# S5 generator: additions moved between VectorE, GpSimd and accumulating DMAs

## The chip, the core and the metric

The kernel runs on one NeuronCore of a Trainium2 chip. The metric is the device time of one launch in microseconds (us). Three runs of the kernel before gave 1716.67, 1719.01 and 1724.01 us, with a median of 1719.01 us. The profiled execution took 1714.45 us. Engines are named as in the profile: PE is TensorE (PEld its weight load), DVE is VectorE, ACT is ScalarE, POOL is GpSimd and SP is SyncE, which issues most of the DMAs.

## The reference, cut to what matters

The reference is one step of a four-layer trunk over 384 tokens (128 of a context, 256 of a sample): an S5 layer, a retention layer, a Hyena layer and a second S5 layer. The change lies in the S5 layers, nearly all of it in the first.

```python
# s5_branch: per layer j; 64 groups of 16 channels, state of 64 complex lanes, two directions
proj = h @ w_in
u, gate = proj[..., :1024], proj[..., 1024:]
bb = f * b                       # complex; f from lam and the step
bu = einsum('blgh,gph->blgp', u, bb)
h[t] = a * h[t-1] + bu[t]        # scan over time, forwards and backwards
y = Re(einsum('blgp,ghp->blgh', h, c)) + d_skip * u
g = gelu(y)
y = g * sigmoid(g @ w_glu + b_glu)
out = (y * silu(gate)) @ w_out
```

## The kernel before, in words

Time is cut into 48 chunks of 8 steps, for each group of channels. Inside a chunk the layer is a small Toeplitz matrix (`Tm`, read back from the scratch array `kd`). Between chunks the state is carried by a recurrence. So for each of 16 "half blocks" (`hb`, four groups each) a generator makes three things out of tables of powers (`B1`, `BI`, `F1`, `FI`): the state input matrices `BP`, which PE transposes into `PB`, the rows of the Toeplitz matrix `Kc`, and the state output matrices `CP`. Each of these is a complex product that `expand` (L625) makes for one direction as two multiplications and one addition over a 128x512 tile: `out = c1*x0` (L629), `t = c2*x1` (L630), `out = out + t` (L631). The second product goes to the ring `xt`. The addition goes through the helper `gstt` to POOL, and so shows in the profile under the helper's line, L134.

The first S5 layer (`j == 0`) runs in these stretches, in this order:

1. **Generator and input projection** (L807 to L822, after the string `PLAN0`). `get_p` calls `gen_b1` (L637) and `gen_b2` (L654) for each half block. DVE multiplies, POOL adds, PE makes the Toeplitz rows (L663) and the transposes (L669), ACT copies out, DVE adds the skip term to `Kc` (L674, L675). Between them the four U weights (1 MB each) are split into a high and a low part (`unit`, L156: ACT casts `wh`, DVE or POOL subtracts to get `wl`, as `sub_any` shares it out) and multiplied with the normalised input `h`. `h` itself is split by `put` (L174), whose subtraction `hl` runs on POOL here (`adanorm(i, hpool, G)`). Six of the 16 `CP` (`SPL`) are made here as well, in a single buffer, and spilled to the scratch array `cpd` by a DMA that POOL issues (L645).
2. **Recurrences** (`recur`, L768). Two halves of the state (`Xs`, q = 0 and 1), for each of 47 dependent steps of five DVE instructions over 128x64 (L790 to L794). Meanwhile PE works through the gate projection (`dense`, L834), whose low parts are all made by POOL (`pool_share[0] = PSG`, which is 3).
3. **Read-out** (L858 to L904). For eight channel blocks m, PE adds three products, one with `Tm` (L878) and two with `CP` (L879, L880), then ACT and DVE apply GELU. The ten `CP` that were not spilled are generated here by `gen_c` (L682): those of m = 0 and 1 (`CPG` is 2) wholly on POOL, the others with DVE multiplications and POOL additions. The other six are loaded back. `xt` has two buffers here and three in the first stretch, and `CP` has six.
4. **GLU and output projection** (L924 to L927), then the retention layer, in which the matrices of the second S5 layer are generated bit by bit, with additions on POOL.

The order of instructions on each engine is fixed when the program is built, by a scheduler that works from its own timeline of the program. Each engine takes its instructions strictly in that order, so an instruction that waits holds back all that stand behind it.

Of the kernel before, what the change touches and what calls it, by code (L numbers as in the profile page):

```python
# [14 lines left out]
OP = mybir.AluOpType  # L15
# [19 lines left out]
RB = 7  # L35
NBC = 2
NH = 2
CPG = 2
RB1 = 10
CP1 = 6  # L40
QS = ("gpsimd", "gpsimd")
# [22 lines left out]
PS0 = 1  # L64
# [41 lines left out]
def hybrid_trunk(ctx: ExitStack, tc: tile.TileContext, I, O, dbg=None, layers=(0, 1, 2, 3)):  # L106
    nc = tc.nc
    V, S, G, TE = nc.vector, nc.scalar, nc.gpsimd, nc.tensor
# [13 lines left out]
    def psm():  # L122
        return pm.tile([128, 512], F32, tag="m", name="psm")
# [9 lines left out]
    def gstt(out, a, b, op):  # L133
        G.tensor_tensor(out, a, b, op=op)  # L134
# [7 lines left out]
    pool_share = [1]  # L142
# [275 lines left out]
    def first_ssq():  # L418
        pss = ssq["first"] = [psm() for _ in range(3)]
        for fb in range(NB):  # L420
            sq = t384("sq")
            S.activation(sq, xT[:, fb, :], AF.Square)
            for t in range(3):
                TE.matmul(pss[t][:, :2], sq[:, t * 128:(t + 1) * 128], ones[:, 0:2], start=fb == 0, stop=fb == NB - 1)
# [197 lines left out]
            defer.extend(steps)  # L622
        return dict(B1=B1, BI=BI, F1=F1, FI=FI, sgn=sgn, dsk=dsk, dmask=dmask)

    def expand(out, rot, T1, T2, x, sl, l0, bufs, eng):  # L625
        c1 = T1[:, sl, l0:l0 + 4].rearrange("p e l -> p l e").unsqueeze(3).to_broadcast([128, 4, 8, 16])
        c2 = T2[:, sl, l0:l0 + 4].rearrange("p e l -> p l e").unsqueeze(3).to_broadcast([128, 4, 8, 16])
        t = rot.tile([128, 4, 8, 16], F32, tag="xt", name="xt", bufs=bufs)
        eng.tensor_tensor(out, c1, x[:, 0].unsqueeze(2).to_broadcast([128, 4, 8, 16]), op=OP.mult)  # L629
        eng.tensor_tensor(t, c2, x[:, 1].unsqueeze(2).to_broadcast([128, 4, 8, 16]), op=OP.mult)  # L630
        gstt(out, out, t, OP.add)  # L631

    def expand_c(CP, rot, tb, xc, hb, xb, eng):
        for d in range(2):
            expand(CP[:, d], rot, tb["B1"], tb["BI"], xc[:, d], slice(1, 9) if d == 0 else slice(8, 0, -1), d * 64 + hb * 4, xb, eng)

    def gen_b1(j, hb, tb, rot, xb=3, nb=1, spill=False):  # L637
        if hb % nb == 0:
            tb["bc"] = rot.tile([128, nb, 2, 2, 2, 4, 16], F32, tag="bc", name="bc", bufs=2)
            (nc.gpsimd if hb > 2 else nc.sync).dma_start(tb["bc"], I["s5bc"][j, hb // 4, :, hb % 4:hb % 4 + nb])  # L640
        rb, xc = tb["bc"][:, hb % nb, 0], tb["bc"][:, hb % nb, 1]
        if spill:
            CP = rot.tile([128, 2, 4, 8, 16], F32, tag="CP", name="CP", bufs=1)
            expand_c(CP, rot, tb, xc, hb, xb, V)
            getattr(nc, SPQ).dma_start(I["cpd"][hb], CP.rearrange("p d g e c -> p (d g e c)"))  # L645
        S.activation(xc, xc, AF.Copy, scale=tb["sgn"][:, 1:2])
        BPs = []
        for d in range(2):
            BP = rot.tile([128, 4, 8, 16], F32, tag="BP", name="BP", bufs=max(xb, 2))
            expand(BP, rot, tb["F1"], tb["FI"], rb[:, d], slice(7, None, -1) if d == 0 else slice(0, 8), d * 64 + hb * 4, xb, V)  # L650
            BPs.append(BP)
        return BPs, xc

    def gen_b2(j, hb, tb, rot, ops, ring=None):  # L654
        BPs, xc = ops
        PB = (ring or rot).tile([128, 4, 2, 128], F32, tag="PB", name="PB")
        psk = psm()
        bps = [[BP[:, g].rearrange("p a b -> p (a b)") for g in range(4)] for BP in BPs]
        last = None
        for d in range(2):  # L660
            xcf = xc[:, d].rearrange("p a b c -> p (a b c)")
            for g in range(4):
                last = TE.matmul(psk[32 * g:32 * g + 32, d * 128:(d + 1) * 128], xcf[:, g * 16:g * 16 + 32], bps[d][g],  # L663
                                 start=True, stop=True)
        with tc.issue_after(last.ins):
            for d in range(2):
                ps = psm()
                for g in range(4):
                    TE.transpose(ps[:, g * 128:(g + 1) * 128], bps[d][g], ident)  # L669
                S.copy(PB[:, :, d, :], ps.rearrange("p (g c) -> p g c", c=128))  # L670
        Kc = rot.tile([128, 240], F32, tag="Kc", name="Kc")
        S.copy(Kc[:, 0:128], psk[:, 0:128])
        S.copy(Kc[:, 128:240], psk[:, 144:256])
        V.tensor_add(Kc[:, 112:128], Kc[:, 112:128], psk[:, 128:144])  # L674
        V.scalar_tensor_tensor(Kc[:, 112:128], tb["dmask"], tb["dsk"][:, hb:hb + 1], Kc[:, 112:128], op0=OP.mult, op1=OP.add)  # L675
        kdm = I["kd"][j * 8 + hb // 2]
        nc.scalar.dma_start(bass.AP(tensor=kdm.tensor, offset=kdm.offset + (hb % 2) * 960, ap=[[240, 4], [1920, 32], [1, 240]]), Kc)
        if ring is None:
            nc.scalar.dma_start(I["pbd"][hb], PB.rearrange("p g d c -> p (g d c)"))
        return PB  # L680

    def gen_c(j, hb, tb, rot, CP, xb, eng=V):  # L682
        xc = rot.tile([128, 2, 2, 4, 16], F32, tag="xc", name="xc")
        nc.sync.dma_start(xc, I["s5bc"][j, hb // 4, :, hb % 4, 1])
        expand_c(CP, rot, tb, xc, hb, xb, eng)

    def gen_cs(j, hb, tb, rot):
        CP = rot.tile([128, 2, 4, 8, 16], F32, tag="CP", name="CP")
# [7 lines left out]
    def s5(i, j, nxt, begun=lambda: None):  # L696
        def mk(st, name, bufs=1, **kw):
            return st.enter_context(tc.tile_pool(name=f"{name}_{i}", bufs=bufs, reuse_waits="tile", **kw))
# [7 lines left out]
        hpool = mk(ep, "s5h")  # L706
        h0 = load(pool, "h0", I["s5h0"][j], eng=nc.scalar)
        if j == 0:
# [3 lines left out]
            with ExitStack() as e2:  # L712
                tb = gen_setup(j, tpool, fpool, mk(e2, "s5p"))
        if i == 0:
            first_ssq()
        h = adanorm(i, hpool, G)
        if j == 1:
            gates = deque(mods(i, 8, 12))
            for _ in range(KN3):
# [87 lines left out]
        for op in (PLAN0, PLAN1)[j].split():  # L807
            n = int(op[1:])
            if op[0] == "A":
                ahead(n)  # L810
            elif op[0] == "U":
                if j == 0:
                    pool_share[0] = PS0 if n == 0 else 1
                firstmajor(i, weight(I["s5_w_in"][j, n]), h, u_epi, 2 * n)
                if n == 0:
                    begun()
            elif op[0] == "P":
                use_p(n)
            elif op[0] == "R":
                recur(n)  # L820
            else:
                tick(n)  # L822
# [17 lines left out]
        rot = mk(e2, "s5c", 2)  # L840
# [17 lines left out]
        for m in range(8):  # L858
            CP = []
            for r in range(2):  # L860
                c = rot.tile([128, 2, 4, 8, 16], F32, tag="CP", name="CP", bufs=CPB if j == 0 else CP1)
                if j == 0 and 2 * m + r not in SPL:
                    gen_c(j, 2 * m + r, tb, rot, c, 2, G if m < CPG else V)
                else:
                    (CQ if j else nc.sync).dma_start(c.rearrange("p d g e c -> p (d g e c)"), I["cpd"][2 * m + r])
                CP.append(c)
# [539 lines left out]
    rb, _ = rstd_bcast()  # L1406
    rs = t384("rs")
    S.copy(rs, rb[:, :T])
    for fb in range(NB):
        t = xT[:, fb, :]  # L1410
# [164 lines left out]
```

## Time and profile before

| | |
|---|---|
| median of three runs | 1719.01 us |
| profiled execution, its own time | 1714.45 us |
| its span on the core | 1712.6 us |
| PE busy | 1500.0 us (88%), 10370 matmuls |
| DVE busy | 1323.1 us (77%), 3065 instructions |
| ACT busy | 686.5 us (40%) |
| POOL busy | 760.9 us (44%), 542 instructions |
| DMA | 253.02 MB, mean 148 GB/s |

The span is the time from the first to the last instruction of the program. The profiled execution's own time is 1.85 us longer than its span. Busy times are shares of that span. They are averages over stretches with different limits: the first S5 layer lies between about 28 and 475 us, the retention layer up to about 760 us, the Hyena layer up to about 1350 us, and the second S5 layer fills the rest.

### The profile page before, as it was taken

How to read it: one execution, taken by the hardware profiler on the slowest of the kernel's cores; microseconds unless marked ns; L12 is line 12 of the kernel's file. 1: busy time of each engine (PE TensorE's matmuls, PEld its weight loads, DVE VectorE, ACT ScalarE, POOL GpSimd, SP SyncE). 2: the span in 40 equal slices, each digit the busy share in tenths (PEclk: the TensorE clock that was granted, in tenths of full speed). 3: DMA queues.
4: the chain of work that ended last, by engine and by line, in shares of the span. 5: the costliest groups of instructions: out<-in, count | busy, mean ns of one | idle time of the engine just before them, and what ended most of it. 6: DMA issues, size and time to landing. Idle time of an engine off the chain costs nothing. (4 is left out here: it accounts for less than half of the span.)

```text
span 1712.6 us, 27808 instructions
## 1 busy us (share of the span) xinstructions
PE 1500.0 (88%) x10370; PEld 1330.8 (78%) x10370; DVE 1323.1 (77%) x3065; ACT 686.5 (40%) x1275; POOL 760.9 (44%) x542
## 2 busy tenths in 40 slices
PE   5788664998779999999979999999999998976996
PEld 3466454877679888889969988989999797775996
DVE  8986999889596776765867888888798764399355
ACT  2434320333324343334445545455454444521343
POOL 2866262424165657461225566556666131230221
PEclk9888796998889999999989999999999999987998
DMA  8476273554545555542432222222222463755431
GB/s 343 134 239 218 64 180 115 191 173 168 194 165 177 172 206 177 191 177 88 163 126 96 96 74 96 96 90 81 96 90 76 147 234 109 230 151 177 125 123 62
DMA packets 103199, 253.02 MB, mean 148 GB/s; under 512 B 28023, under 2 KB 68056, under 8 KB 83480
## 3 DMA queue, kind: packets, MB, share of 16 engines
q1 hardware_dynamic: 80768, 200.12, 35.8%
q0 software_dynamic: 7376, 26.48, 4.7%
q10 hardware_dynamic: 14920, 24.65, 4.0%
q8 instruction: 82, 1.34, 0.3%
q14 instruction: 53, 0.43, 0.1%
HBM read 220.37 MB, written 30.83 MB: 147 GB/s over the span
## 5 line engine op out<-in xcount | busy, mean ns | idle before, releaser
L134 POOL TENSOR_TENSOR wl<-wr,wh 128x1024 fp32r<-128x1024 f32 (+2 forms) x101 | 253.2, 2507 | 361.6 <-ACT wh L162 309.5
L162 ACT CAST wh<-wr 128x1024 fp32r<-128x1024 f32 (+4 forms) x211 | 215.5, 1029 | 339.4 <-PE psd L139 222.2
L139 PE MATMUL psd<-hh,wh 128*128 128x384 f32 x880 | 309.2, 353 | 47.8 <-DVE sgate L532 23.1
L139 PE MATMUL psd<-hh,wl 128*128 128x384 f32 x880 | 307.0, 350 | 15.9 <-DVE wl L149 8.2
L139 PE MATMUL psd<-hl,wh 128*128 128x384 f32 x880 | 307.1, 349 | 5.8 <-DVE hl L470 4.8
L139 PEld LDWEIGHTS psd<-hh,wh 128*128 128x128 f32 x880 | 171.4, 195 | 60.8 <-issue 44.2
L149 DVE TENSOR_TENSOR wl<-wr,wh 128x1024 fp32r<-128x1024 f32 (+3 forms) x110 | 144.6, 1316 | 71.6 <-ACT wh L162 71.2
L139 PEld LDWEIGHTS psd<-hh,wl 128*128 128x128 f32 x880 | 170.5, 194 | 25.5 <-DVE wl L149 10.1
L139 PEld LDWEIGHTS psd<-hl,wh 128*128 128x128 f32 x880 | 171.2, 195 | 16.4 <-DVE hl L470 7.5
L134 POOL TENSOR_TENSOR CP<-CP,xt 128x512 f32<-128x512 f32 x64 | 95.6, 1499 | 90.6 <-DVE xt L630 72.2
L134 POOL TENSOR_TENSOR BP<-BP,xt 128x512 f32<-128x512 f32 x64 | 96.6, 1514 | 80.0 <-DVE xt L630 30.6
L139 PE MATMUL psd<-wh,hh 128*128 128x256 f32 x384 | 111.7, 295 | 4.7 <-ACT k L1074 4.1
L139 PE MATMUL psd<-wl,hh 128*128 128x256 f32 x384 | 111.5, 292 | 4.1 <-POOL wl L134 2.2
L139 PE MATMUL psd<-wh,hl 128*128 128x256 f32 x384 | 110.5, 289 | 0.0
L139 PE MATMUL psd<-zb,wh 128*128 128x384 f32 x240 | 81.1, 339 | 0.0
L139 PEld LDWEIGHTS psd<-wl,hh 128*128 128x128 f32 x384 | 75.7, 197 | 5.9 <-DVE wl L149 3.0
L139 PEld LDWEIGHTS psd<-wh,hh 128*128 128x128 f32 x384 | 74.7, 196 | 6.6 <-ACT k L1074 4.9
L630 DVE TENSOR_TENSOR xt<-FI,bc 128x512 f32<-128x512 f32 x64 | 64.4, 1018 | 16.8 <-POOL CP L134 9.1
L139 PEld LDWEIGHTS psd<-wh,hl 128*128 128x128 f32 x384 | 75.5, 197 | 0.3 <-issue 0.2
L791 DVE TENSOR_TENSOR m<-X,A 128x64 f32<-128x64 f32 x188 | 69.4, 369 | 0.0
L630 DVE TENSOR_TENSOR xt<-BI,xc 128x512 f32<-128x512 f32 x44 | 47.4, 1077 | 26.6 <-POOL CP L134 18.4
L379 PE MATMUL psn<-wr,sgc 128*32 128x256 f32 x640 | 52.5, 404 | 16.3 <-DMA wr<-in_mod_w_dram 9.9
(388 smaller groups left out, 4020.9 us busy)
## 6 DMA issues: line engine op xcount, KB each, us to landing
wr<-in_mod_w_dram SPq DMA_DIRECT2D x40, 1024.0 KB
wr<-in_hy_w_in_dram SPq DMA_DIRECT2D x32, 1024.0 KB
wr<-in_ret_w_in_dram SPq DMA_DIRECT2D x24, 1024.0 KB
wr<-in_s_w_in_dram SPq DMA_DIRECT2D x16, 1024.0 KB
wm<-in_mod_w_dram SPq DMA_DIRECT2D x8, 1024.0 KB
Tt<-scratch_kd_dram SPq DMA_DIRECT2D x128, 64.0 KB
wr<-in_s_w_glu_dram SPq DMA_DIRECT2D x8, 1024.0 KB
wr<-in_s_w_out_dram SPq DMA_DIRECT2D x8, 1024.0 KB
```

The lines of the kernel that those rows point to most:

```text
L134: G.tensor_tensor(out, a, b, op=op)
L139: TE.matmul(out, lhs[a], rhs[b], start=start and i == 0, stop=stop and i == len(combos) - 1)
L149: V.tensor_sub(out, a, b)
L162: S.copy(hi, ap)
L379: TE.matmul(ps[q * 32:(q + 1) * 32, :256], sg[:, kb, 6 - 2 * u:38 - 2 * u], raw[:, kb, :], start=u == 0 and k2 == 0, stop=u == 3 and k2 == 1)
L630: eng.tensor_tensor(t, c2, x[:, 1].unsqueeze(2).to_broadcast([128, 4, 8, 16]), op=OP.mult)
L791: V.tensor_mul(m1, cur, A1)
```

## The change

There are five edits.

- `expand` is told where its addition runs: on an engine that is named, or, with `None`, in an accumulating DMA that POOL issues (`dma_start(out, t, accum_op=add)`, SBUF to SBUF, 128x512 float32, 256 KB).
- The `BP` additions of the first S5 layer run on DVE; those made in the retention layer for the second S5 layer stay on POOL (`G if j else V`).
- The `CP` additions of the first S5 layer, spilled or not, become accumulating DMAs. The multiplications that POOL made for m = 0 and 1 go to DVE, and `CPG` is gone. `gen_cs`, which makes the `CP` of the second layer, keeps its additions on POOL.
- The first layer's `hl` subtractions run on DVE, and so do all eight U splits (`pool_share[0] = 0`).
- `Kc`: ACT copies 112 columns rather than 128, and DVE makes the diagonal block from PSUM directly (first the skip term, then the second direction's block).

```diff
-    def expand(out, rot, T1, T2, x, sl, l0, bufs, eng):
+    def expand(out, rot, T1, T2, x, sl, l0, bufs, eng, add):
...
         eng.tensor_tensor(out, c1, x[:, 0].unsqueeze(2).to_broadcast([128, 4, 8, 16]), op=OP.mult)
         eng.tensor_tensor(t, c2, x[:, 1].unsqueeze(2).to_broadcast([128, 4, 8, 16]), op=OP.mult)
-        gstt(out, out, t, OP.add)
+        if add is None:
+            nc.gpsimd.dma_start(out, t, accum_op=OP.add)
+        else:
+            add.tensor_tensor(out, out, t, op=OP.add)
...
-            expand_c(CP, rot, tb, xc, hb, xb, V)
+            expand_c(CP, rot, tb, xc, hb, xb, V, None)
...
-            expand(BP, rot, tb["F1"], tb["FI"], rb[:, d], slice(7, None, -1) if d == 0 else slice(0, 8), d * 64 + hb * 4, xb, V)
+            expand(BP, rot, tb["F1"], tb["FI"], rb[:, d], slice(7, None, -1) if d == 0 else slice(0, 8), d * 64 + hb * 4, xb, V, G if j else V)
...
-        S.copy(Kc[:, 0:128], psk[:, 0:128])
+        S.copy(Kc[:, 0:112], psk[:, 0:112])
         S.copy(Kc[:, 128:240], psk[:, 144:256])
+        V.scalar_tensor_tensor(Kc[:, 112:128], tb["dmask"], tb["dsk"][:, hb:hb + 1], psk[:, 112:128], op0=OP.mult, op1=OP.add)
         V.tensor_add(Kc[:, 112:128], Kc[:, 112:128], psk[:, 128:144])
-        V.scalar_tensor_tensor(Kc[:, 112:128], tb["dmask"], tb["dsk"][:, hb:hb + 1], Kc[:, 112:128], op0=OP.mult, op1=OP.add)
...
-    def gen_c(j, hb, tb, rot, CP, xb, eng=V):
+    def gen_c(j, hb, tb, rot, CP, xb, eng=V, add=G):
...
-        h = adanorm(i, hpool, G)
+        h = adanorm(i, hpool, V if j == 0 else G)
...
-                    pool_share[0] = PS0 if n == 0 else 1
+                    pool_share[0] = 0
...
-                    gen_c(j, 2 * m + r, tb, rot, c, 2, G if m < CPG else V)
+                    gen_c(j, 2 * m + r, tb, rot, c, 2, V, None)
```

On POOL, at the start of the generator (right behind the last product of the power tables, `pb`), the row before is full of additions (`BP`, `CP`), `h` splits (`hl`) and weight splits (`wl`):

```order
L134 TENSOR_TENSOR BP<-BP,xt 128x512 x3
L176 TENSOR_TENSOR hl<-hf,hh 128x384 x3
L134 TENSOR_TENSOR BP<-BP,xt 128x512 x2
L176 TENSOR_TENSOR hl<-hf,hh 128x384 x3
L640 DMA bc<-in_s5bc_dram 128x1024
L134 TENSOR_TENSOR BP<-BP,xt 128x512 x2
L176 TENSOR_TENSOR hl<-hf,hh 128x384 x2
L134 TENSOR_TENSOR CP<-CP,xt 128x512 x2
```

With the change POOL at the same place only issues DMAs: loads of `bc` (the generator's input), accumulations into `CP`, and the spill behind each pair of them:

```order
L642 DMA bc<-in_s5bc_dram 128x1024
L631 DMA CP<-xt 128x512 x2
L642 DMA bc<-in_s5bc_dram 128x1024
L647 DMA scratch_cpd_dram<-CP 128x1024
L631 DMA CP<-xt 128x512 x2
L647 DMA scratch_cpd_dram<-CP 128x1024
```

All POOL arithmetic of that stretch has moved to DVE, but for the additions into `CP`, which have become DMAs in POOL's row.

On DVE, in the first stretch of the generator, the row before has only products (`xt`), the normalisation (`ht`) and the skip term (`Kc`):

```order
L395 SCALAR_TENSOR_TENSOR sc_145<-mod_144,vec 128x16
L630 TENSOR_TENSOR xt<-FI,bc 128x512
L460 TENSOR_TENSOR ht<-xT,psm 128x384
L630 TENSOR_TENSOR xt<-FI,bc 128x512
L460 TENSOR_TENSOR ht<-xT,psm 128x384
```

With the change the additions into `BP` and the `hl` subtractions stand between them:

```order
L394 SCALAR_TENSOR_TENSOR sc_145<-mod_144,vec 128x16
L629 TENSOR_TENSOR xt<-FI,bc 128x512
L633 TENSOR_TENSOR BP<-BP,xt 128x512 x2
L459 TENSOR_TENSOR ht<-xT,psm 128x384
L633 TENSOR_TENSOR BP<-BP,xt 128x512
L629 TENSOR_TENSOR xt<-FI,bc 128x512
L175 TENSOR_TENSOR hl<-hf,hh 128x384
```

Between the start of this stretch and the first instruction of the first recurrence the row of DVE grows by 28 additions, 8 subtractions and 2 weight splits.

On DVE, in the recurrences (`X_200` and `X_201` are the two halves of the state, `sw` and `m` their products), the row before reaches the first products of `CP` only near the end of the second recurrence, behind the last gate block:

```order
L532 SCALAR_TENSOR_TENSOR sgate<-silu,psd 128x384
L790 STREAM_SHUFFLE sw<-X_201 128x64
L791 TENSOR_TENSOR m_2510<-X_201,A_399 128x64
L793 TENSOR_TENSOR sw<-sw,A_399 128x64
L792 TENSOR_TENSOR X_201<-X_201,m_2510 128x2x32
L794 TENSOR_TENSOR X_201<-X_201,sw 128x2x32
L790 STREAM_SHUFFLE sw<-X_201 128x64
L791 TENSOR_TENSOR m_2517<-X_201,A_399 128x64
L793 TENSOR_TENSOR sw<-sw,A_399 128x64
L792 TENSOR_TENSOR X_201<-X_201,m_2517 128x2x32
L794 TENSOR_TENSOR X_201<-X_201,sw 128x2x32
L629 TENSOR_TENSOR CP<-B_224,xc 128x512 x2
```

With the change they begin while both recurrences are still running, before the fourth gate block:

```order
L792 STREAM_SHUFFLE sw<-X_200 128x64
L793 TENSOR_TENSOR m_1874<-X_200,A_399 128x64
L628 TENSOR_TENSOR CP<-B_224,xc 128x512
L629 TENSOR_TENSOR xt<-BI,xc 128x512
L796 TENSOR_TENSOR X_201<-X_201,sw 128x2x32
L628 TENSOR_TENSOR CP<-B_224,xc 128x512
L629 TENSOR_TENSOR xt<-BI,xc 128x512
L796 TENSOR_TENSOR X_201<-X_201,sw 128x2x32
L795 TENSOR_TENSOR sw<-sw,A_399 128x64
L794 TENSOR_TENSOR X_200<-X_200,m_1874 128x2x32
L531 SCALAR_TENSOR_TENSOR sgate<-silu,psd 128x384
```

Up to the last instruction of the second recurrence the row before has 8 products of this kind; with the change it has 39, four additions into `BP` and four GELU blocks in place of two.

## Rows read from the trace of the kernel before

**Rows 1.** Windows: stretch; length, busy PE, PEld, DVE, ACT, POOL; clock, DMA share, GB/s.

```profile
47.00:178.00 131.00, 99.70 (x844) 70.72 (x844) 108.33 (x132) 55.22 (x126) 90.52 (x64) 0.85 0.62 202
178.00:231.00 53.00, 41.70 (x322) 31.45 (x323) 53.00 (x301) 16.68 (x33) 11.11 (x8) 0.83 0.31 88
231.00:267.00 36.00, 12.99 (x83) 10.62 (x81) 36.00 (x45) 6.16 (x11) 35.81 (x28) 0.78 0.55 127
267.00:318.00 51.00, 37.28 (x302) 32.03 (x303) 50.09 (x268) 8.59 (x17) 7.71 (x6) 0.82 0.54 163
318.00:355.00 37.00, 36.47 (x351) 30.81 (x348) 25.68 (x52) 11.77 (x23) 16.48 (x12) 1.00 0.59 201
```

**Rows 2.** Timeline, DVE: start and length; the recurrences' first and last instruction.

```profile
178.29 1.24 DVE L773 COPY XF<-X 128x32 f32<-128x32 f32 x1
...
317.82 0.26 DVE L794 TENSOR_TENSOR X<-X,sw 128x64 f32<-128x64 f32 x1
```

**Rows 3.** Groups, DVE, 47 to 178 us: busy, mean ns | idle before.

```profile
L630 DVE TENSOR_TENSOR xt<-FI,bc 128x512 f32<-128x512 f32 x29 | 35.1, 1239 | 0.7 <-POOL BP L134 0.7
L629 DVE TENSOR_TENSOR BP<-F,bc 128x512 f32<-128x512 f32 x30 | 26.8, 914 | 7.3 <-PE psm L669 7.3
L630 DVE TENSOR_TENSOR xt<-BI,bc 128x512 f32<-128x512 f32 x12 | 14.2, 1197 | 1.3 <-DMA bc<-in_s5bc_dram 1.3
L675 DVE SCALAR_TENSOR_TENSOR Kc<-dmask,dsk,Kc 128x16 f32<-128x16 f32 x13 | 13.9, 1071 | 0.1
L629 DVE TENSOR_TENSOR CP<-B,bc 128x512 f32<-128x512 f32 x12 | 8.0, 682 | 9.0 <-DMA bc<-in_s5bc_dram 9.0
L149 DVE TENSOR_TENSOR wl<-wr,wh 128x1024 fp32r<-128x1024 f32 x4 | 6.1, 1519 | 0.0
```

**Rows 4.** One line's instructions, whole span: ns min/median/max, first and last start.

```profile
L630 DVE TENSOR_TENSOR xt<-FI,bc x64: 675/693/3122, 51.4 to 747.3; 128x512 f32<-128x512 f32 x64
...
L629 DVE TENSOR_TENSOR BP<-F,bc x64: 644/684/1780, 47.3 to 741.3; 128x512 f32<-128x512 f32 x64
...
L675 DVE SCALAR_TENSOR_TENSOR Kc<-dmask,dsk,Kc x32: 214/366/3540, 60.6 to 755.9; 128x16 f32<-128x16 f32 x32
...
L176 DVE TENSOR_TENSOR zl<-zz,zh x16: 546/554/1026, 374.1 to 1666.4; 128x384 fp32r<-128x384 f32 x16
```

**Rows 5.** Groups, POOL, 47 to 178 us.

```profile
L134 POOL TENSOR_TENSOR BP<-BP,xt 128x512 f32<-128x512 f32 x29 | 45.7, 1585 | 25.7 <-DVE BP L629 14.6 <-DVE xt L630 6.0 <-DVE Kc L674 2.8
```

**Rows 6.** Groups, DVE, 231 to 266 us, while POOL is busy throughout.

```profile
L794 DVE TENSOR_TENSOR X<-X,sw 128x64 f32<-128x64 f32 x8 | 12.1, 1559 | 0.0
L793 DVE TENSOR_TENSOR sw<-sw,A 128x64 f32<-128x64 f32 x7 | 9.7, 1387 | 0.0
L791 DVE TENSOR_TENSOR m<-X,A 128x64 f32<-128x64 f32 x7 | 7.9, 1135 | 0.0
L792 DVE TENSOR_TENSOR X<-X,m 128x64 f32<-128x64 f32 x6 | 7.0, 1168 | 0.0
```

**Rows 7.** Groups, DVE, 268 to 289 us, while POOL is idle.

```profile
L794 DVE TENSOR_TENSOR X<-X,sw 128x64 f32<-128x64 f32 x24 | 5.5, 258 | 0.0
```

**Rows 8.** Groups, POOL, 178 to 290 us.

```profile
L134 POOL TENSOR_TENSOR wl<-wr,wh 128x1024 fp32r<-128x1024 f32 x6 | 14.4, 2399 | 24.9 <-ACT wh L162 24.9
L134 POOL TENSOR_TENSOR CP<-CP,xt 128x512 f32<-128x512 f32 x8 | 10.0, 1268 | 0.0
...
L630 POOL TENSOR_TENSOR xt<-BI,xc 128x512 f32<-128x512 f32 x8 | 8.7, 1106 | 0.0
L629 POOL TENSOR_TENSOR CP<-B,xc 128x512 f32<-128x512 f32 x8 | 8.7, 1108 | 9.8 <-DMA xc<-in_s5bc_dram 9.8
L134 POOL TENSOR_TENSOR BP<-BP,xt 128x512 f32<-128x512 f32 x4 | 5.5, 1369 | 7.8 <-DVE sw L793 5.2 <-DVE X L780 1.2 <-PE psm L663 0.8
```

**Rows 9.** POOL's spill DMAs of `CP`: issue time in ns, and time to landing.

```profile
L645 POOL DMA_DIRECT2D scratch_cpd_dram<-CP x6: 571/576/576, 83.5 to 179.4; - x6
...
DMA to landing us min/median/max: 2.9/5.2/8.8
```

More of the change, by code (lines that the diff above doesn't have):

```diff
@@ L37 @@
 NH = 2
-CPG = 2
 RB1 = 10
@@ L630, in expand, with expand_c @@
         eng.tensor_tensor(t, c2, x[:, 1].unsqueeze(2).to_broadcast([128, 4, 8, 16]), op=OP.mult)
-        gstt(out, out, t, OP.add)
-    def expand_c(CP, rot, tb, xc, hb, xb, eng):
+        if add is None:
+            nc.gpsimd.dma_start(out, t, accum_op=OP.add)
+        else:
+            add.tensor_tensor(out, out, t, op=OP.add)
+    def expand_c(CP, rot, tb, xc, hb, xb, eng, add):
         for d in range(2):
-            expand(CP[:, d], rot, tb["B1"], tb["BI"], xc[:, d], slice(1, 9) if d == 0 else slice(8, 0, -1), d * 64 + hb * 4, xb, eng)
+            expand(CP[:, d], rot, tb["B1"], tb["BI"], xc[:, d], slice(1, 9) if d == 0 else slice(8, 0, -1), d * 64 + hb * 4, xb, eng, add)
     def gen_b1(j, hb, tb, rot, xb=3, nb=1, spill=False):
@@ L680, in gen_b2 @@
         return PB
-    def gen_c(j, hb, tb, rot, CP, xb, eng=V):
+    def gen_c(j, hb, tb, rot, CP, xb, eng=V, add=G):
         xc = rot.tile([128, 2, 2, 4, 16], F32, tag="xc", name="xc")
         nc.sync.dma_start(xc, I["s5bc"][j, hb // 4, :, hb % 4, 1])
-        expand_c(CP, rot, tb, xc, hb, xb, eng)
+        expand_c(CP, rot, tb, xc, hb, xb, eng, add)
     def gen_cs(j, hb, tb, rot):
```

## The prediction, written before the changed kernel was run

> **What bounds the kernel now.** I read the windows first, by stretch of the first S5 layer. From 47 us, where the generator starts, to 178 us, DVE is busy for 108.3 of 131 us and PE for 99.7 [rows 1]. From 178 to 267 us DVE never rests (53 of 53 and 36 of 36 us), and PE has only 13 of 36 us in the last part. From 267 to 318 us DVE again has 50 of 51. Only from 318 to 355 us is PE the bound (36.5 of 37). The timeline gives the two marks in between: the first recurrence starts at 178.29 us, the second ends at 317.82 us, so together they last 140 us [rows 2]. The layer's read-out cannot end before them. So the path is DVE from 47 to 318 us and PE after that.
>
> The groups by line, read second, say that much of DVE's busy time is no work. In the generator the second product takes 1239 ns in the mean, and the small skip-term instruction 1071 ns [rows 3]; the same lines have a median of 693 and a minimum of 214 ns over the span [rows 4]. In the recurrences the contrast is clearest: while POOL is busy 35.8 of 36 us, an addition over 128x64 takes 1559 ns, and when POOL rests it takes 258 ns [rows 1, 6, 7]. DVE instructions with two SBUF operands wait here for POOL's arithmetic, roughly one POOL instruction each. So a microsecond of arithmetic taken from POOL can free DVE time, although POOL itself is never the bound.
>
> **The change part by part: generator, 47 to 178 us.** What goes is POOL's arithmetic there. The DVE time lost beside it is (1239-693)x29 = 15.8 for the second products, (914-684)x30 = 6.9 for the first, (1197-693)x12 = 6.0 for those of CP and (1071-214)x13 = 11.1 us for the skip term [rows 3, 4]: 40 us. What comes to DVE: 28 additions into BP at 0.69 us (no DVE addition of this shape is in the trace; the two products have the same shape and operands) = 19.3; 8 hl subtractions, for which the nearest row is zl with 0.554 us [rows 4] = 4.4; 2 weight splits at most 1.52 us [rows 3] = 3.0. Together 27. On POOL the same additions took 1.59 us each [rows 5]. Bounds for a DVE addition: 0.64 us (the fastest product) and 0.91 us (the first product's mean beside POOL), which is 18 to 26 us for the 28.
>
> The skip term's new order costs nothing by itself: two small instructions as before, and ACT's copy is shorter.
>
> What else comes is waiting. The 12 CP additions of this stretch become DMAs, and three things stand behind them: the next product that needs a buffer of the ring xt (three), the spill on POOL's queue, and the next spilled CP, which has one buffer. A product that waits holds the whole row of DVE behind it: additions into BP, for which PE's transposes wait, and then the input to the recurrences. No accumulating DMA is in the trace. The nearest row is POOL's spill of 512 KB, issued in 0.58 us and landed after 2.9 / 5.2 / 8.8 us [rows 9]. An accumulation moves half the bytes but reads its destination too, so I take 5.2 + 0.6 = 5.8 us, with bounds 3.5 and 9.4. Adding up DVE's new row at quiet durations, with a product held until the accumulation three products earlier has landed, gives waits of 0 / 5 / 21 us. The single CP buffer: accumulation and spill take 11.6 us, and 20 or so instructions of 0.69 us (14 us) stand between one spilled CP and the next, so it is hidden; at 9.4 us each it would lack 5 us, five times, mostly inside the 21.
>
> Generator: -40 + 27 + 5 = -8 us. PE's 99.7 us of 131 would let it go 31 us lower, so that floor does not decide.
>
> [...]
>
> **Recurrences, 178 to 318 us.** What goes: POOL's additions and products of CP and the last additions into BP. Between 231 and 266 us DVE lost (1559-258)x8 + (1387-258)x7 + (1135-258)x7 + (1168-258)x6 = 10.4 + 7.9 + 6.1 + 5.5 = 30 us [rows 6, 7]. But the weight splits of the gate projection stay on POOL: six of them have 14.4 us of this stretch, some 9 of them among the 35.8 busy us [rows 1, 8]. So 30 x 26/36 = 22 goes. The four BP additions (5.5 us [rows 8]) and the first CP additions after 290 us give back about 5 us each. Together 32.
>
> What comes: 31 more products here at 0.69 us = 21.4, of which 16 were POOL's and 15 stood behind the recurrences; 4 additions into BP = 2.8; two more GELU blocks, three instructions of 0.55 us each = 3.3. Together 27.5. The wait at xt, with two buffers here, comes out of the same count at 0 / 5 / 28 us; I take 6, since POOL issues some of these DMAs behind gate splits that wait for ACT [rows 8]. What stands behind such a product on DVE is a step of the recurrence, and with it PE's read-out. Recurrences: -32 + 27.5 + 6 = +1.5 us, that is, no gain: they carry work of the read-out instead.
>
> **Read-out, 318 to 355 us.** PE bounds it, with or without the change. But PE's new row has transposes of Tt and modulation products ahead of the end of the recurrences which stood behind it, and 36 GLU matmuls moved in front of the read-out's end. 36 at 1500/10370 = 0.145 us (the table of busy times) are 5 us done early; the moved transposes and products I estimate at 3 us, from the 37 us of a full PE [rows 1]. Read-out: -8 us.
>
> **Sum.** -8 + 1.5 - 8 = -14.5 us, against the profiled execution: 1714.45 - 14.5 = 1700 us. The median of the runs was 1719, 4.6 us above that execution, so I predict 1719 - 14.5, rounded to 1704 us. The second layer's generator is left as it was, and after 355 us I count nothing: the rows there are reordered, but no term can be read.
>
> **The rivals.** First, slower: **the accumulations land late**. The place is the second product of CP in the row of DVE, in the generator and in the recurrences; the price is the wait at xt. At the spill's worst row, 8.8 + 0.6 us [rows 9], it is 21 + 28 in place of 11 us, a sum of +23 us, 1742 us. It decides from about 7.5 us per accumulation, where the sum is zero. For it: 32 of these DMAs with two reads and one write beside a queue load of 0.5 to 0.6 [rows 1], and POOL's in-order row. Against it: xt has slack in most places, and half the bytes of the spill.
> [...]
>
> Second, **the freed time is not the path's**: what DVE gains in the generator is waited out elsewhere, since DVE already idles 23 of 131 us there for PE, ACT and loads (7.3 us for transposes, 10.3 for bc [rows 3]). If the generator's 8 us and half of the read-out's are lost, 2.5 us are left: 1716 us, no change.
>
> Third, **a larger gain**: accumulations land within 3.5 us, the waits are zero, and the generator's idle time shrinks as POOL's row no longer delays bc by additions. That is -25.5 us and up to 10 us of the 10.3 us idle for bc: -30 to -36 us, 1683 to 1689 us.
>
> **How the numbers follow.** The forecast (-9 to -25 us, 1694 to 1710 us) gets 0.40, the larger gain 0.17, no change 0.21, late landings 0.22. What a measurement of this kernel can tell from no change is about 0.5%, 8.6 us. So faster is 0.57, the same 0.21, slower 0.22. The range for 8 times in 10 is 1680 to 1742 us: the larger gain to its middle, and the slower rival to its computed time. The forecast's own range is 1694 to 1710 us.
>
> **What would show it.** Right: DVE's second product near 0.7 us in the generator, the 128x64 additions near 0.26 us but beside wl, the first recurrence starting near 170 us, the second ending near 311 us, the read-out ending near 340 us. Accumulations landing at about 5 us. Wrong: DVE idle in front of L629 with a DMA of CP as the releaser, for more than some 25 us in all; or DVE additions that take much more than 0.7 us with POOL idle, which would mean that the time was not lost to POOL's arithmetic.

## The result, and the profile after

The changed kernel took 1695.87 us (median of four runs) against 1718.48 us of the kernel before beside it: a ratio of 0.9884, with a 95% interval of 0.9856 to 0.9912. A later repetition gave 0.9857 (0.9829 to 0.9885). So it is 1.2 to 1.4% faster, some 20 to 25 us. The profiled execution had a span of 1693.3 us, 19.3 us below that of before. The four runs spread from 1689.64 to 1700.13 us, so a mark read from one profiled execution is good to a few us only.

First the windows of the changed kernel, with the columns of [rows 1]: the generator, the recurrences, the rest of the read-out, GLU and output projection, and the start of the retention layer up to its first query-key product.

```profile
46.00:167.00 121.00, 94.28 (x836) 68.28 (x840) 88.16 (x167) 53.24 (x121) 15.01 (x21) 0.85 0.74 222
167.00:325.30 158.30, 110.02 (x864) 86.69 (x852) 141.58 (x652) 40.76 (x78) 40.75 (x33) 0.83 0.75 197
325.30:357.50 32.20, 32.12 (x266) 29.43 (x270) 12.10 (x44) 7.76 (x13) 6.15 (x5) 0.92 0.39 123
357.50:444.30 86.80, 76.43 (x460) 65.53 (x464) 75.19 (x177) 35.57 (x60) 28.65 (x30) 0.96 0.41 148
444.30:493.00 48.70, 36.50 (x243) 28.86 (x243) 42.61 (x86) 18.04 (x40) 23.73 (x17) 0.82 0.55 201
```

The last two stretches in the kernel before:

```profile
355.00:453.00 98.00, 86.75 (x522) 76.00 (x526) 81.67 (x194) 35.93 (x62) 31.92 (x31) 0.93 0.45 153
453.00:507.00 54.00, 37.75 (x243) 30.88 (x231) 45.61 (x87) 17.75 (x40) 26.77 (x21) 0.78 0.56 187
```

The generator is 10 us shorter, and DVE is busy in it for 88 us instead of 108 [rows 1]. But the recurrences last 158 us instead of 140. The timeline of DVE has the two marks that answer to [rows 2]:

```profile
167.12 0.18 DVE L775 COPY XF<-X 128x32 f32<-128x32 f32 x1
...
325.05 0.28 DVE L796 TENSOR_TENSOR X<-X,sw 128x64 f32<-128x64 f32 x1
```

The first recurrence starts 11 us earlier than before, the second ends 7 us later. The read-out ends at 357.5 us, where before it was 354.6. So at that point nothing is gained. The gain comes behind it: GLU and output projection take 86.8 us instead of 98, the stretch up to the first query-key product 48.7 instead of 54.

The groups of DVE in the generator (46 to 167 us), to be held against [rows 3]:

```profile
L628 DVE TENSOR_TENSOR BP<-F,bc 128x512 f32<-128x512 f32 x30 | 19.9, 684 | 3.2 <-PE psm L671 3.2
L629 DVE TENSOR_TENSOR xt<-FI,bc 128x512 f32<-128x512 f32 x29 | 19.5, 687 | 9.2 <-DMA CP<-xt 9.0
L633 DVE TENSOR_TENSOR BP<-BP,xt 128x512 f32<-128x512 f32 x28 | 18.8, 684 | 0.1
L629 DVE TENSOR_TENSOR xt<-BI,bc 128x512 f32<-128x512 f32 x12 | 8.1, 685 | 0.7 <-DMA CP<-xt 0.7
...
L676 DVE SCALAR_TENSOR_TENSOR Kc<-dmask,dsk,psm 128x16 f32<-128x16 f32 x13 | 2.9, 224 | 9.8 <-ACT Kc L675 9.8
```

The second product is down from 1239 to 687 ns, the skip term from 1071 to 224 ns. In their place stand waits: 9.7 us for accumulations into `CP`, 9.8 us for ACT's copy of `Kc` (4.2 us before).

The accumulating DMAs themselves, by their line: the issue on POOL in ns (minimum, median, maximum), and the time to landing. They answer to [rows 9].

```profile
L631 POOL DMA_DIRECT2D CP<-xt x32: 839/862/1202, 71.2 to 334.4; - x32
...
DMA to landing us min/median/max: 3.4/7.2/12.5
```

They land after 7.2 us where I took 5.8. Behind the generator DVE waits for them once more, and PE waits for the loads of modulation weights, 2.1 us in the kernel before. The waits of DVE from 167 to 326 us and of PE from 46 to 360 us (us in all, times, longest):

```profile
DVE xt L629 <- DMA CP<-xt: 10.8, 7, 2.7
```

```profile
PE psn L378 <- DMA wr<-in_mod_w_dram: 29.9, 6, 8.0
```

### The profile page after: what moved, and what is told of

Read it like the earlier page. It is cut to its first block, busy times and chain, and to the rows that moved or that the text cites. A ratio compares the mean times of both kernels' runs of the same rounds, so it can differ in the third digit from the quotient of the medians.

```text
span 1693.3 us, 27807 instructions
## 1 busy us (share of the span) xinstructions
PE 1488.7 (88%) x10370; PEld 1320.6 (78%) x10370; DVE 1288.4 (76%) x3123; ACT 688.8 (41%) x1275; POOL 660.6 (39%) x484
## 5 line engine op out<-in xcount | busy, mean ns | idle before, releaser
L133 POOL TENSOR_TENSOR wl<-wr,wh 128x1024 fp32r<-128x1024 f32 (+2 forms) x99 | 248.3, 2513 | 322.2 <-ACT wh L161 294.4
L138 PEld LDWEIGHTS psd<-hh,wl 128*128 128x128 f32 x880 | 169.1, 192 | 20.1 <-POOL wl L133 10.5
L378 PE MATMUL psn<-wr,sgc 128*32 128x256 f32 x640 | 58.3, 450 | 45.4 <-DMA wr<-in_mod_w_dram 37.9
L629 DVE TENSOR_TENSOR xt<-BI,xc 128x512 f32<-128x512 f32 x52 | 45.2, 870 | 37.0 <-POOL CP L633 16.6
L378 PEld LDWEIGHTS psn<-wr,sgc 128*32 128x32 f32 x640 | 20.0, 121 | 67.3 <-DMA wr<-in_mod_w_dram 41.2
L633 POOL TENSOR_TENSOR BP<-BP,xt 128x512 f32<-128x512 f32 x32 | 46.0, 1437 | 63.7 <-DVE xt L629 37.7
L629 DVE TENSOR_TENSOR xt<-FI,bc 128x512 f32<-128x512 f32 x64 | 48.8, 768 | 26.7 <-DMA CP<-xt 9.0
L631 POOL DMA_DIRECT2D CP<-xt x32 | 27.6, 905 | 101.0 <-DVE X L796 28.7
```

The lines of the kernel that those rows point to most:

```text
L138: TE.matmul(out, lhs[a], rhs[b], start=start and i == 0, stop=stop and i == len(combos) - 1)
L378: TE.matmul(ps[q * 32:(q + 1) * 32, :256], sg[:, kb, 6 - 2 * u:38 - 2 * u], raw[:, kb, :], start=u == 0 and k2 == 0, stop=u == 3 and k2 == 1)
L631: nc.gpsimd.dma_start(out, t, accum_op=OP.add)
L633: add.tensor_tensor(out, out, t, op=OP.add)
```

## The experiments

Two views are held against each other in all of them: the ratio, and four marks of the profiled execution in us: the start of the first recurrence, the end of the recurrences, the end of the read-out, and the last matmul of the layer's output projection ("layer"). "Rest" is the time from there to the end of the last arithmetic instruction, which is one of DVE, 4 to 7 us before the end of the span. The ratios of one block were taken on one chip against the same runs of the kernel before (the blocks are separated by empty rows).

| kernel | ratio (95% interval) | start | rec. end | read-out | layer | rest |
|---|---|---|---|---|---|---|
| before | 1 | 178.3 | 318.1 | 354.6 | 452.7 | 1255.2 |
| changed | 0.9884 (0.9856-0.9912) | 167.1 | 325.3 | 357.5 | 444.3 | 1244.6 |
| | | | | | | |
| cp_dve | 0.9809 (0.9779-0.9839) | 163.3 | 313.5 | 335.3 | 423.3 | 1247.6 |
| bp_pool | 0.9899 (0.9874-0.9924) | 180.2 | 331.7 | 361.6 | 449.9 | 1245.1 |
| split_pool | 0.9864 (0.9836-0.9891) | 163.8 | 316.9 | 344.9 | 436.8 | 1248.3 |
| gate_dve | 0.9837 (0.9809-0.9865) | 169.6 | 313.6 | 341.2 | 429.3 | 1257.6 |
| | | | | | | |
| cp_pool | 0.9876 (0.9863-0.9890) | 167.0 | 324.6 | 351.0 | 441.3 | 1248.2 |
| cp_gen_dma | 0.9911 (0.9897-0.9925) | 168.4 | 330.6 | 352.5 | 441.2 | 1251.6 |
| cp_read_dma | 0.9867 (0.9854-0.9881) | 164.9 | 312.2 | 339.8 | 432.1 | 1250.2 |
| cp_dve_gate | 0.9841 (0.9828-0.9855) | 162.6 | 317.8 | 342.3 | 430.0 | 1248.5 |
| | | | | | | |
| before_again | 0.9988 (0.9975-1.0001) | 179.4 | 320.2 | 356.7 | 455.1 | 1255.8 |
| after_again | 0.9857 (0.9829-0.9885) | 167.6 | 325.2 | 357.8 | 445.7 | 1247.3 |
| kc_alone | 0.9918 (0.9898-0.9939) | 177.2 | 320.1 | 353.0 | 447.9 | 1248.7 |
| xt_read3 | 0.9841 (0.9816-0.9865) | 167.0 | 319.6 | 344.3 | 433.5 | 1251.8 |

**Additions into CP on DVE instead of by DMA (cp_dve).**

```diff
-            expand_c(CP, rot, tb, xc, hb, xb, V, None)
+            expand_c(CP, rot, tb, xc, hb, xb, V, V)
-                    gen_c(j, 2 * m + r, tb, rot, c, 2, V, None)
+                    gen_c(j, 2 * m + r, tb, rot, c, 2, V, V)
```

> The additions into CP of the first layer run on DVE instead of in accumulating DMAs; all else is as in the changed kernel. Theory A (the gain is DVE time that was lost beside POOL's arithmetic; where the addition goes, as long as it leaves POOL, matters little): the generator's row of DVE grows by 12 x 0.69 = 8 us and loses 12 us of waits for CP, the recurrences' and read-out's grow by 20 x 0.69 = 14 us and lose 18 us. First recurrence starts at 163 to 168 us, time 1690 to 1700 us, against 1696 of the changed kernel. Theory B (the gain is that an addition left all engines for the DMA queues): DVE gets 22 us longer for nothing, time 1708 to 1718 us.

1684.88 us, 0.9809. The start is as theory A has it, and the time is below even its range; theory B falls. The DMAs are the part of the change that costs: the marks from the recurrences' end to the layer's end come 12 to 22 us earlier without them (in an execution of 1677.77 us, 7 us less than the median of the six). Of its waits, PE's for modulation weights shrinks with them:

```profile
PE psn L378 <- DMA wr<-in_mod_w_dram: 12.3, 7, 3.4
```

By its ratio this is the fastest of all kernels here, though the intervals of gate_dve, xt_read3 and cp_dve_gate overlap with its own. The ratio lies below both of the changed kernel; the intervals meet only at the edge of the second.

**Additions into BP back on POOL (bp_pool).**

```diff
-            expand(BP, ..., xb, V, G if j else V)
+            expand(BP, ..., xb, V, G)
```

> The additions into BP of the first layer go back to POOL; all else is as in the changed kernel. Theory A: each POOL addition costs DVE about 0.9 us (45 us over the 51 POOL instructions of the kernel before), in place of 0.69 us of its own, so 28 x 0.2 = 6 us; the second product goes back to 1.1 to 1.2 us in the mean; the first recurrence starts at 171 to 175 us (167 in the changed kernel), time 1700 to 1704 us. Theory B: the additions into BP are not what the gain came from, 1694 to 1698 us.

1699.78 us, 0.9899. The start is at 180.2 us, 13 us later than in the changed kernel and not 4 to 8 as theory A had it. The groups of DVE from 50 to 180 us say why:

```profile
L629 DVE TENSOR_TENSOR xt<-FI,bc 128x512 f32<-128x512 f32 x29 | 27.0, 938 | 11.4 <-POOL BP L633 6.9 <-DMA CP<-xt 4.5
L628 DVE TENSOR_TENSOR BP<-F,bc 128x512 f32<-128x512 f32 x27 | 21.1, 797 | 1.8 <-PE psm L671 1.7
```

The longer products come back (938 ns against 687), and POOL's additions also hold the ring `xt`: DVE waits for their results (6.9 us here). So the additions into BP are what shortened the generator. Of the 13 us only 3 to 7 are left in the whole (by the two ratios of the changed kernel).

**The h splits and first U splits back on POOL (split_pool).**

```diff
-        h = adanorm(i, hpool, V if j == 0 else G)
+        h = adanorm(i, hpool, G)
-                    pool_share[0] = 0
+                    pool_share[0] = PS0 if n == 0 else 1
```

> The h splits and two of the U splits of the first layer go back to POOL; all else is as in the changed kernel. Theory A: 8 + 2 to 4 POOL instructions beside DVE cost it 0.9 us each, about 10 us, and save 4.4 + 3 to 4 us of DVE's own: +2 us in the generator, time 1695 to 1700 us. Rival C (the gain came with the order of work on PE, which gets its first U input sooner): the splits decide that order, so most of the gain goes, 1708 to 1718 us.

1693.05 us, 0.9864. This is below theory A's range and far from rival C's. That part of the change brings nothing that can be measured.

**The gate's weight splits on DVE (gate_dve).**

```diff
-        pool_share[0] = PSG
+        pool_share[0] = PSG if j else 0
```

> The weight splits of the first layer's gate projection and of the read-out's stretch, all on POOL in the changed kernel, run on DVE; all else is as there. Theory A: DVE still loses 25 us between 167 and 325 us, nearly all in instructions over 128x64, and the only POOL arithmetic left there are these splits (9 of 2.4 us between 47 and 360 us). On DVE they take 1.22 us each: -22 + 11 = -11 us in the recurrences, their end at 313 to 318 us instead of 325, time 1684 to 1692 us. Rival D (PE and the loads of modulation weights bound that stretch by now, with 30 us of waits for such loads in PE's row): the end of the layer does not move, 1693 to 1700 us.

1688.12 us, 0.9837. The recurrences end at 313.6 us, as theory A has it, and the layer ends 15 us earlier than in the changed kernel. But the rest takes 1257.6 us instead of 1244.6 us: most of the gain is given back behind the layer, in code that the edit doesn't touch.

**Additions into CP on POOL (cp_pool).**

```diff
-            expand_c(CP, rot, tb, xc, hb, xb, V, None)
+            expand_c(CP, rot, tb, xc, hb, xb, V, G)
-                    gen_c(j, 2 * m + r, tb, rot, c, 2, V, None)
+                    gen_c(j, 2 * m + r, tb, rot, c, 2, V, G)
```

> The additions into CP of the first layer run on POOL (as in the kernel before, but with the multiplications on DVE); all else is as in the changed kernel (about 1695 us; with the same additions on DVE it was 1685). Theory A': beside POOL's arithmetic DVE loses about 0.62 us for each POOL instruction (19.4 us for 31 in the run with BP's additions on POOL, 32.8 for 53 in the kernel before), no less than the 0.69 us that the addition costs on DVE itself; so POOL is no better place than DVE, but better than a DMA that lands after 7 us: 1683 to 1692 us. Theory B (additions by DMA are worth having against POOL): 1697 to 1706 us.

1694.20 us, 0.9876: between the two ranges, and the same as with the DMAs. For these 32 additions an accumulating DMA is worth no more than POOL, and both are behind DVE. Theory A' put the loss per POOL instruction too low for the kernel before: the 41 DVE instructions that POOL delayed there, between 47 and 178 us, took 44 us longer than quiet ones, 0.83 us for each of 53 POOL instructions. In bp_pool it is 19 us for 30, 0.63 us each.

**The DMAs in the generator alone, and in the read-out alone (cp_gen_dma, cp_read_dma).** Each has one of the two lines of cp_dve.

> The ten CP that are made in the read-out and recurrences add on DVE; the six that are spilled keep their accumulating DMAs. Theory E1 (what the DMAs cost is the wait of a product for the ring xt: 12 us in the generator, 18 us after it, against 8 and 14 us of DVE additions): some 6 us of the 10 to 13 us that the DMAs cost in all, 1686 to 1692 us. Theory E2 (what they cost is that their traffic delays the loads of modulation weights, for which PE waits 30 us in the changed kernel and 12 us without these DMAs, mostly between 250 and 325 us): nearly all of it comes back, 1681 to 1686 us.

> The reverse: the six spilled CP add on DVE in the generator, the ten later ones keep their accumulating DMAs. Theory E1: the generator gives back its share, 4 to 6 us, first recurrence at 163 to 165 us, 1688 to 1692 us. Theory E2: next to nothing comes back, since the later DMAs stay beside the loads, 1692 to 1697 us.

cp_gen_dma took 1700.70 us, 0.9911: above both ranges. cp_read_dma took 1692.12 us, 0.9867: at the border of both, with its start at 164.9 us as E1 has it. Nothing adds up here: with only the DMAs of the generator it is no faster than with all. From the read-out on cp_gen_dma has the same stretches as cp_dve (21.8 us to the end of the read-out); the 17 us between them arise before, 5 us in the generator and 12 us in the recurrences, where all its gate splits fall on POOL (two of cp_dve's are done by then). Why the order came out so stays open. Theory E2 does not hold by PE's waits for modulation weights either (46 to 360 us). cp_gen_dma has none of the later DMAs and waits longer than cp_read_dma, which has all of them; first cp_gen_dma, then cp_read_dma:

```profile
PE psn L378 <- DMA wr<-in_mod_w_dram: 21.9, 9, 7.2
```

```profile
PE psn L378 <- DMA wr<-in_mod_w_dram: 14.5, 6, 5.2
```

cp_pool, which has no accumulating DMA at all, waits 17.9 us.

**Both gains together (cp_dve_gate).** The edits of cp_dve and gate_dve.

> CP's additions on DVE, and the weight splits of the first layer's gate projection on DVE too (the two runs that gained, together). Theory A: no POOL arithmetic is left beside the recurrences but for products with the gate; DVE's loss of 25 us there falls to about 10 as in the run with the gate splits alone, and both gains add up: 1673 to 1680 us. Rival D (PE with its modulation loads bounds the layer once DVE is this much freer, so that the second gain has nothing to shorten): 1682 to 1688 us.

1687.01 us, 0.9841: rival D's range. The two do not add up; it is no faster than cp_dve.

**Both kernels again (after_again, before_again).** No edit.

> The changed kernel once more, unaltered, to see what of its 19 us stays in place from one execution to the next. In the first profile 8 us are gained by the end of the first layer (444.3 us against 452.7) and 11 us after it (1244.6 us from there to the end, against 1255.2). Theory F (the later gain belongs to the program: the order in which instructions of the second layer's generator and the modulation matmuls fall): end of the layer at 443 to 446 us, 1243 to 1247 us from there. Rival G (it is the granted clock of that one execution): the layer ends where it did, and the rest takes anything from 1245 to 1256 us. Time 0.986 to 0.991 of the kernel before.

> The kernel before once more, unaltered. Theory F: the layer ends at 451 to 454 us, 1253 to 1257 us from there. Rival G: from there 1245 to 1256 us, with no fixed place. Ratio 1 within 0.3%.

Ratios 0.9857 and 0.9988. The marks of each kernel come back within 3 us: the layer ends at 445.7 and 455.1 us, the rest takes 1247.3 and 1255.8 us. They lie within 1.1 us of theory F's ranges, but rival G's range for the rest takes them in as well, so the two parts of the rest have to be looked at one by one. Up to the first query-key product 5.3 us are gained in the first pair of executions and 5.9 us in the second. That part comes back, and belongs to the program. From there to the end it is 5.3 us and 2.6 us. PE has the same 7536 matmuls there; in the order before, before_again, changed, after_again:

```profile
506.60:1707.90 1201.30, 1119.56 (x7536) 1030.72 (x7534) 881.82 (x1860) 525.21 (x949) 528.06 (x356) 0.97 0.41 134
509.50:1710.90 1201.40, 1118.13 (x7536) 1029.33 (x7534) 882.72 (x1859) 524.59 (x948) 527.01 (x355) 0.97 0.41 134
492.90:1688.90 1196.00, 1113.70 (x7536) 1024.84 (x7534) 887.69 (x1860) 523.92 (x947) 533.39 (x359) 0.98 0.41 135
494.20:1693.00 1198.80, 1117.49 (x7536) 1031.58 (x7534) 885.75 (x1860) 523.86 (x947) 532.75 (x359) 0.97 0.41 134
```

At the clock of 0.97 PE is busy for as long as before, to within 2 us. So half of the 5.3 us can be the granted clock of one execution. What recurs, in front of the query-key product, is in the rows. These are two windows of 8 us, from 23 to 7 us before the first query-key product, in the kernel before:

```profile
484.00:492.00 8.00, 4.83 (x29) 3.48 (x27) 8.00 (x13) 3.28 (x6) 5.96 (x5) 0.87 0.39 134
492.00:500.00 8.00, 7.85 (x33) 7.61 (x33) 6.64 (x7) 1.33 (x2) 8.00 (x6) 0.71 0.59 201
```

And in the changed kernel:

```profile
470.00:478.00 8.00, 7.15 (x39) 6.51 (x37) 7.50 (x18) 2.45 (x6) 2.41 (x3) 0.99 0.50 186
478.00:486.00 8.00, 7.19 (x44) 6.36 (x45) 7.86 (x9) 1.61 (x3) 7.92 (x7) 1.00 0.18 50
```

Before, PE is idle for 3.2 us of the first window and then works at a granted clock of 0.71: in steps of half a microsecond it is 0.50 from 490 to 496.5 us and 1.00 from 497 us on. That gives 62 matmuls in 16 us. After, the clock is 0.99 and 1.00, and it is 83. The repetitions show the same (0.67 and 1.00 in the second of the windows).

**The skip term's edit alone (kc_alone).** The kernel before with this one edit:

```diff
-        S.copy(Kc[:, 0:128], psk[:, 0:128])
+        S.copy(Kc[:, 0:112], psk[:, 0:112])
+        V.scalar_tensor_tensor(Kc[:, 112:128], ..., psk[:, 112:128], ...)
         V.tensor_add(Kc[:, 112:128], Kc[:, 112:128], psk[:, 128:144])
-        V.scalar_tensor_tensor(Kc[:, 112:128], ..., Kc[:, 112:128], ...)
```

> The kernel before with one of the five edits alone: the skip term reads PSUM instead of SBUF, and ACT copies 112 columns. In the profile of before this instruction waits 11 us in the generator, each time until 29 to 45 ns after the end of a POOL instruction. Theory A (the edit costs and gives nothing by itself): the wait passes to the next DVE instruction with two SBUF operands, since POOL's arithmetic is unaltered; first recurrence at 176 to 181 us, time within 0.3% of the kernel before. Rival K (the skip term's 11 us are gained by its new operand): first recurrence at 166 to 171 us, 0.993 to 0.996 of the kernel before.

1702.51 us, 0.9918: faster by some 14 us, more than either theory allowed. In the generator theory A is right. The instruction itself no longer waits, its maximum is 231 ns over all 32 (line, whole span), where it was 3540 [rows 4]:

```profile
L674 DVE SCALAR_TENSOR_TENSOR Kc<-dmask,dsk,psm x32: 212/219/231, 59.0 to 747.3; 128x16 f32<-128x16 f32 x32
```

Ten of the 32 ran wholly inside a POOL instruction, in 216 to 230 ns; of the 32 in the kernel before, none did. One of the ten, first DVE, then POOL:

```profile
59.01 0.22 DVE L674 SCALAR_TENSOR_TENSOR Kc<-dmask,dsk,psm 128x16 f32<-128x16 f32 x1
...
58.04 2.88 POOL L176 TENSOR_TENSOR hl<-hf,hh 128x384 fp32r<-128x384 f32 x2
```

But others wait in its place (41 delayed DVE instructions between 47 and 178 us, as many as before), and the first recurrence starts where it did. The gain lies behind it: 4 us in the read-out, 3 to 4 us in GLU and output projection, 7 us in the rest. A part of the last is plain: 16 of the 32 instructions stand in the retention layer, where the second layer's matrices are made beside POOL's additions. PE's waits for BP there, in the kernel before (453 to 766 us) and with this edit (448 to 757 us):

```profile
PE psm L663 <- POOL BP L134: 5.9, 5, 2.2
```

```profile
PE psm L663 <- POOL BP L134: 2.3, 5, 0.8
```

In the changed kernel the same wait is 2.1 us. What the other 10 us come from was not settled; no instruction of the read-out or of GLU and output projection is altered, only their order. This one edit alone has more than half of the changed kernel's gain (14 of 20 to 25 us). No run takes it out of the changed kernel, so how much of that gain the other four edits make is open.

**Three xt buffers in the read-out (xt_read3).**

```diff
-                    gen_c(j, 2 * m + r, tb, rot, c, 2, V, None)
+                    gen_c(j, 2 * m + r, tb, rot, c, 3, V, None)
```

> The changed kernel with three xt buffers instead of two for the ten CP made beside the recurrences and the read-out (the generator keeps its three). Theory E1 (what the accumulating DMAs cost there is that a product waits for the ring): the waits for CP behind the generator fall from 18 us to 8 us or less, and with them the end of the recurrences from 325 to 314 to 319 us; 0.982 to 0.986 of the kernel before. Rival H (the DMAs come late in any case, for POOL's row holds them and the queues are full from 250 to 320 us): the wait moves to the next instruction that needs CP, 0.987 to 0.990.

1690.10 us, 0.9841: within E1's range, and the recurrences' end at 319.6 us just above it. The waits from 167 to 360 us fell from 11.7 to 4.8 us, though the DMAs landed no sooner (8.2 us in the median):

```profile
DVE xt L629 <- DMA CP<-xt: 4.8, 4, 2.3
```

So in the recurrences, which end 5.6 us earlier, part of what these DMAs cost is the wait at the ring. In the whole time it is not shown: the interval overlaps that of after_again, taken beside it.

## Why the prediction was right, and where it was not

The direction and about the size are right: -14.5 us forecast, -19 us in the profiles, -20 to -25 us by the ratios. The way to it is right for the generator alone. Of the marks that the prediction named, the first recurrence (near 170) came at 167.1 us; the end of the second (near 311) came at 325.3, the read-out's (near 340) at 357.5. DVE's idle time in front of L629 with `CP` as the releaser is 21.4 us over the span, close to the 25 us that were to show it wrong.

**The mechanism holds.** In the generator of the kernel before, DVE instructions with two SBUF operands waited for POOL's arithmetic, to the end of it: from 47 to 178 us none of them ran wholly inside a POOL instruction (over the whole span twelve did). DVE and POOL near 70 us:

```profile
69.47 3.54 DVE L675 SCALAR_TENSOR_TENSOR Kc<-dmask,dsk,Kc 128x16 f32<-128x16 f32 x1
...
69.49 2.53 POOL L134 TENSOR_TENSOR BP<-BP,xt 128x512 f32<-128x512 f32 x2
71.97 1.00 POOL L176 TENSOR_TENSOR hl<-hf,hh 128x384 fp32r<-128x384 f32 x1
```

The small instruction sits out three POOL instructions in a row and ends at 73.01 us, 0.04 us after the third. In the changed kernel two of the gate's weight splits follow each other on POOL, and two instructions of DVE wait for one each (in brackets POOL's idle time before them):

```profile
170.01 2.12 DVE L793 TENSOR_TENSOR m<-X,A 128x64 f32<-128x64 f32 x1
172.05 2.37 DVE L795 TENSOR_TENSOR sw<-sw,A 128x64 f32<-128x64 f32 x1
...
169.71 4.64 POOL L133 TENSOR_TENSOR wl<-wr,wh 128x1024 fp32r<-128x1024 f32 x2 [5.46 <-ACT wh L161]
```

All 41 delayed instructions in the generator of before end at such a distance from the end of a POOL instruction: 29 to 45 ns for 128x16, 546 to 559 ns for 128x512, 1092 ns for 128x1024. DVE instructions that read one operand from PSUM were not held: of the eight `ht` in this stretch seven ran wholly inside a POOL instruction, in 541 to 543 ns, and so did kc_alone's ten skip terms (216 to 230 ns). One of the 41 has a single SBUF tensor as input and was held all the same, for 1120 ns where the fastest of its line takes 157; why, no run here shows:

```profile
L400 DVE TENSOR_SCALAR gt<-mod 128x16 f32<-128x16 f32 x1 | 1.1, 1120 | 0.0
```

**Generator, -8 us: right (-10), in part because two misses cancel.** DVE's busy time fell by 20 us, where -40 and +27 make 13, and its idle time rose by 10, where I took 5. The additions cost 0.684 us each (0.69 taken), and the lost time went. The waits for accumulations were 9.7 us where I took 5, and ACT's copy of `Kc` is a wait that I did not name. DVE idles 33 of 121 us (23 of 131 before), so part of what it gained is waited out. The 5.8 us per accumulation had the issue in it twice: [rows 9] counts the 5.2 us from the start of the issue. The U splits on DVE are six in this stretch instead of four, 1.22 us each, as counted.

**Recurrences, +1.5 us: wrong (+18).** I counted from the start of each DVE instruction to that of the next. What was added came to 21 us against 27.5 forecast. Two terms were mis-sized. "Together 32" for the lost time that goes was 20: 38 us were lost beside POOL before, and 18 still are (over the five lines of the recurrence, what a step to the next instruction took beyond 0.14 us, the mean of the rest, where it took more than 0.45 us, without idle time). Eight weight splits of the gate fall here, 19.3 us of POOL, and stop DVE for those 18 us, nearly their whole length; I had six with 14.4 us, and counted some 9 us of them. And "I take 6" for the wait at `xt` was 14, `xc` included. -20 + 21 + 14, with 2 us of other waits, is about the +18. gate_dve shows the first (recurrences 14 us shorter), xt_read3 and cp_dve the second.

**Read-out, -8 us: half right (-4), and put in the wrong place.** That PE does later work early is right, in larger measure: 188 modulation matmuls stand in the recurrences where there were 112, and 36 GLU matmuls before the read-out's end. By the lines of PE in that stretch, before and after:

```profile
L379 PE MATMUL psn<-wr,sgc x112: 379/379/637, 215.1 to 305.6; 128*32 128x256 f32 x112
```

```profile
L378 PE MATMUL psn<-wr,sgc x188: 379/403/636, 166.6 to 320.3; 128*32 128x256 f32 x188
```

Each takes about 0.4 us, but they overlap. In busy time of PE, before and after (the columns after the length are PE, PEld, clock, DMA share, GB/s):

```profile
178.00:318.00 140.00, 8.15 (x112) 3.20 (x112) 0.81 0.46 126
```

```profile
167.00:325.30 158.30, 16.93 (x188) 5.62 (x176) 0.83 0.75 197
```

That is 9 us more of PE's work in the recurrences, and the 36 GLU matmuls in the read-out are another 7 us (5 taken). This work is missing behind the read-out: GLU and output projection have 62 matmuls fewer, PE is busy there for 10 us less, and the stretch takes 11 us less. But not all of the longer recurrences is made good so: cp_dve ends them 12 us earlier and the layer 21 us earlier.

**After 355 us, "I count nothing": wrong.** From the end of the read-out to the end of the program 22 us are gained, the whole of the result: 11 in GLU and output projection, 5 up to the first query-key product, 5 after that (in the repetitions 10.5, 6 and 2.6). Also, "the second layer's generator is left as it was" overlooked that the skip term's edit applies there too. And "the skip term's new order costs nothing by itself" is true of the generator, but alone it moves the time by 0.8%, and why is for the most part open.

**The rivals.** The landing of 7.2 us is close to the 7.5 us from which "late landings" was to make a sum of zero. The mechanism was there (21.4 us of waits in all, against the 11 taken), and cp_dve shows its price: 0.5 to 0.75% of the time, 8 to 13 us, by the two ratios of the changed kernel. But the zero point rested on the wrong terms behind it. "The freed time is not the path's" is what bp_pool and gate_dve show: 13 us at the start of the recurrences and 15 us at the end of the layer became 3 to 7 and 3 to 8 us in the whole.

The range took in the result, but by luck: the sum was near for two errors of opposite sign, +17 in the recurrences and -22 behind the read-out.

## What to carry to other kernels

An addition on POOL is not free beside a busy DVE: in the generator here each POOL instruction cost DVE 0.6 to 0.8 us, about the 0.68 us that the addition takes on DVE itself, and beside the recurrences a weight split cost it nearly its whole 2.4 us. An accumulating DMA was no way around it: with 7 us to landing it gained nothing over POOL, and a deeper ring cut the waits for it from 11.7 to 4.8 us without a gain in the whole time that is clear of noise. Where a scheduler plans the whole program, compare marks at the ends of stages and repeat both kernels: the skip term's small edit moved 14 us here, half of it in stages that the edit doesn't touch, and gains from single edits did not add up.

## What the runs showed of the hardware that was not expected

An accumulating DMA takes more of the DMA engines than its bytes say. Queues of the changed kernel from 250 to 325 us (packets, MB, share of 16 engines):

```profile
q1 hardware_dynamic: 7575, 14.74, 65.6%
q0 software_dynamic: 2158, 3.93, 31.1%
```

The second queue holds just 15 accumulations of 256 KB: 7.9% of the engines' time per MB, against 4.5% for the first queue, which is nearly all loads. The engines are full there (97%). Whether PE's weights come late for that is not shown: in cp_pool the share over the same 75 us is 55%, and PE still waits 17.9 us for them (46 to 360 us). The landing of the accumulations (3.4 / 7.2 / 12.5 us) is above that of the spills (2.9 / 5.2 / 8.8 us [rows 9]), which carry twice the bytes.
